# RWKV's inverses in blocks of sixteen rows on VectorE, the samples' blocks turned on chip

## The chip, the cores and the metric

One Trainium2 chip, one core. The metric is the device time of one execution in microseconds (us); the kernel before has a median of 1343.44 us over 3 runs. Engines are called by their names in the profile: PE (TensorE's matmuls), PEld (its weight loads), DVE (VectorE), ACT (ScalarE), POOL (GpSimd), SP (SyncE, from whose queue nearly all DMAs are issued). Each engine takes its instructions in order.

## The reference: one step of a two-layer recurrent decoder

A prompt of 256 tokens and 8 samples of 8 tokens each (320 columns together) run through two layers with the same float32 weights. Layer 0 mixes with 4 GLA heads and 16 RWKV-7 heads, layer 1 with RG-LRU blocks and Mamba-2 heads; each layer ends with a gated feed-forward part of width 2816. Outputs are the tokens' final vectors and all new recurrent states.

The change touches RWKV-7 alone. Its reference is a scan over time, per head with a 64x64 state S:

```python
sa = einsum('bhij,bhj->bhi', s, -kk_t)
s = s * w_t + sa[..., None] * (kk_t * a_t) + v_t[..., None] * k_t
y = einsum('bhij,bhj->bhi', s, r_t)
```

In chunks of 64 tokens this becomes products of matrices, if for each head and chunk a 64x64 triangular system is solved: with A the strictly triangular matrix of the products of the chunk's vectors kk and kk * a (with decays), the chunk needs T = (I + A)^-1. The prompt has 4 chunks and 16 heads, that is 64 inverses of 64x64; the 8 samples have blocks of 8x8, 128 of them.

## The kernel before, in words

All activations lie with channels on the 128 partitions and the 320 tokens along the free axis. A projection (`lin`, L98) streams 320 columns against 128x128 weight tiles; float32 weights and activations are each split into a rounded high part and a remainder, and three matmuls are added up. ScalarE makes the weights' high part (`whi`, L87), VectorE the remainder (`wlo`, L92), from tiles that the sync queue loads (`wraw`, three buffers). So VectorE's queue feeds every projection.

Layer 0 takes the 16 RWKV heads in four quarters of four. Each quarter has `rwkv_front` (six projections, decays, and for two pairs of heads the products of the chunk's vectors), `rwkv_back` (samples, inverse, scan over the four chunks, norm), and beside them one GLA head. The front of the next quarter and the GLA head are written behind a quarter's back; the order on each engine is then laid out at compile time by a scheduler with estimated durations, and does not change at run time. Most of a quarter's tiles (`GA`, `GS`, `BKt`, `SV`, `G`) have one buffer: the next quarter's are written when this quarter's scan has read them.

The path that the change touches, per quarter (4 heads x 4 chunks = 16 matrices):

- `rwkv_pair` writes the 16 matrices into `GA` (128 partitions, 64 columns of time, 32 places for matrices), each twice: VectorE multiplies the product with the mask, GpSimd copies it to a second place (L653 to L655). `GS` takes the samples' blocks.
- `rwkv_inverse_s` (samples): VectorE sums the masked blocks into 64x32 values (L686), two DMAs through DRAM (`usd`) turn them so that 32 partitions hold one 8x8 block each, `solve` substitutes back in 7 pairs of a product and a sum, three DMAs through DRAM (`xsd`) turn the result back, and two products with a mask (`mkb`) spread it to `Ts` (`rts`).
- `rwkv_inverse` (prompt): two block transposes (L712) put each matrix's two diagonal blocks of 32 rows on partitions, one block per partition; ScalarE copies them to the other 64 partitions (L87), so that each partition half solves for half of the columns. Odd rows are folded into even ones (two instructions on 128x512), so that two rows go at a time: 16 steps, each a product `T` (L92) and a sum over its last axis into `X` (L726), from 32 to 512 columns. The result is transposed back (L728), copied into `Tt` by VectorE and GpSimd (eight copies, L738), and the block below the diagonal is joined on TensorE: two transposes (L743), 16 products of 32x32 with `GA`, ScalarE's evacuation, 16 products with `Tt`, ScalarE's evacuation into `Tt`.
- `rwkv_prompt` then runs the four chunks with `Tt` on TensorE.

A float32 matmul of this kernel shows as two records of PE.

Of the kernel before, what the change touches and what calls it, by code (L numbers as in the profile page):

```python
# [23 lines left out]
NB = 8  # L24
# [7 lines left out]
class Net:  # L32
# [370 lines left out]
    def masks0(self, pool):  # L403
        nc = self.nc

        mp = self.t(pool, [P, 2, 64], "mkp")
        msm = self.t(pool, [P, 2, 64], "mks")
        nc.gpsimd.memset(mp, 1.0)
        nc.gpsimd.memset(msm, 1.0)
        for b in (0, 64):  # L410
            for m in (mp, msm):
                self.sel(m[b:b + 64], [[1, 2], [1, 64]], -1, -1)
            self.sel(msm[b:b + 64].rearrange("p a (b t) -> p a b t", t=8), [[0, 2], [-8, 8], [0, 8]], 0, 1)
        self.mkp, self.mks = mp, msm
# [12 lines left out]
        self.eye = self.t(pool, [P, 32, 8], "eye")  # L427
        e1 = self.t(self.m0, [P, 512], "T", 1)[:, :256].rearrange("p (s c) -> p s c", c=8)
        for d, e in enumerate((self.eye, e1)):
            nc.gpsimd.memset(e, 0.0)  # L430
            for r in range(0, P, 32):
                x = e[r:r + 32]
                self.sel(x, [[1, 32], [-1, 8]], -16 * (r // 64) - 8 * d, 0, 1.0, OP.not_equal)
                self.sel(x, [[0, 32], [0, 8]], -16 if d else 15, 1 if d else -1)
        self.tt(self.eye, self.eye, e1, OP.add, nc.gpsimd)
# [102 lines left out]
    def rwkv_front(self, quarter, h, W):  # L538
        q = type("Quarter", (), {})()
        q.n = quarter  # L540
        t = lambda tag, w, n=1: self.t(self.m0, [P, 2, w], tag, self.BUFS.get(tag, n))
        q.AR = t("AR", 640).rearrange("p m (c a t) -> p m c a t", c=5, a=2)
        q.BKt = t("BKt", 640).rearrange("p m (c k) -> p m c k", c=5)
        q.SV = t("SV", 640).rearrange("p m (c k) -> p m c k", c=5)
        q.G = t("G", 640).rearrange("p m (c h t) -> p m c h t", c=5, h=2)

        q.GA = self.t(self.m0, [P, 64, 32], "GA", self.BUFS.get("GA", 1))
        q.GS = self.t(self.m0, [P, 2, 2, 64], "GS", 1)
        q.BV = t("BV", 320).rearrange("p m (c v) -> p m c v", c=5)
# [27 lines left out]
    def rwkv_pair(self, q, m, i, h, W, kr, kn):  # L577
# [60 lines left out]
        for lo, n in ((0, 4), (4, 1)):  # L638
# [7 lines left out]
            for hh in range(2):  # L646
# [31 lines left out]

    def rwkv_inverse_s(self, q):

        nc = self.nc
        usd = self.t(self.dr, [2, 2, 64, 8], "usd", 2)
        xsd = self.t(self.dr, [2, 2, 64, 8], "xsd", 2)
        t = self.t(self.m0, [P, 256], "ti", 1)
        us, U, X, xr, T = (t[:64, 0:32], t[:32, 64:128], t[:32, 128:192], t[:, 32:48], t[:32, 192:256])
# [7 lines left out]
        x3 = xr.rearrange("p (m t) -> p m t", m=2)  # L693
        for hh in range(2):
            self.dq.dma_start(out=x3[hh * 64:hh * 64 + 64], in_=xsd[:, hh].rearrange("m s t -> s m t"))
        q.Ts = self.t(self.m0, [P, 2, 64], "rts", 1)
        for m in range(2):
            self.tt(q.Ts[:, m, :].rearrange("p (b t) -> p b t", t=8),
                    x3[:, m, :].unsqueeze(1).to_broadcast([P, 8, 8]),
                    self.mkb.unsqueeze(2).to_broadcast([P, 8, 8]), OP.mult)  # L700

    def rwkv_inverse(self, q):

        nc = self.nc
        U = self.t(self.m0, [P, 32, 32], "U", 1)
        X = self.t(self.m0, [P, 32, 8], "X", 1)
# [7 lines left out]
        t3 = T.rearrange("p (t m) -> p t m", m=16)  # L716
        self.tt(t3, U[:, :, 1::2], Uf[:, 32::66].unsqueeze(1).to_broadcast([P, 32, 16]), OP.mult)
        self.tt(U[:, :, 0::2], U[:, :, 0::2], t3, OP.subtract)
        nc.gpsimd.memset(Uf[:, 0::33], -1.0)  # L719
        nc.gpsimd.tensor_copy(X, self.eye)  # L720
        for i in range(30, -1, -2):
            k = 32 - i
# [4 lines left out]
        XT = U.rearrange("p t s -> p (t s)")[:, :256].rearrange("p (t g) -> p t g", g=32)  # L727
        nc.vector.transpose(XT, X.rearrange("p s t -> p t s"))  # L728
        q.Tt = Tt = self.t(self.m0, [P, 2, 4, 64], "Tt", 1)
        for a in range(2):  # L730
            for b in range(2):
                src = XT[a * 64 + b * 32:a * 64 + b * 32 + 32].rearrange("p t (b g h) -> p h g b t", b=2, h=2)
                for hh in range(2):
                    o = hh * 64 + b * 32
                    c = b * 32 + a * 16
                    d = Tt[o:o + 32].rearrange("p m c t -> p (m c) t")[:, :, c:c + 16]
                    d = d.rearrange("p g (b t) -> p g b t", b=2)
                    (nc.gpsimd if hh else nc.vector).tensor_copy(d, src[:, hh])  # L738
# [939 lines left out]
```

## Time and profile before

| | |
|---|---|
| timed runs | 1343.44 us median (1339.86, 1343.44, 1346.21) |
| profiled execution | 1337.24 us, span 1335.5 us, mean granted clock 0.961 |
| busy | PE 93%, PEld 84%, DVE 67%, ACT 53%, POOL 15% |
| chain that ended last | PE 74%, DVE 12%, ACT 6%, issue 4%, DMA 2%, POOL 2% |
| on that chain, by line | T L92 1%, X L726 1%, wlo L92 2% |
| T L92, X L726 | 64 each, 44.9 and 27.5 us busy |

Busy shares are means over the whole span. Layer 0's four quarters lie between 95 and 500 us; the two feed-forward parts, in which PE runs almost without a gap, at 557 to 800 and from 1040 on. The chain is followed back from the last instruction, so a line's share there is time that it held the end up, in this execution. A busy PE counts pipelined matmuls.

### The profile page before, as it was taken

The numbers are of one execution on the slowest core, as the hardware profiler recorded it, in microseconds if no ns is written. First come the engines' busy times: TensorE is split into PE (matmuls) and PEld (weight loads), VectorE is DVE, ScalarE is ACT, GpSimd is POOL, SyncE is SP. The second block draws the span as 40 slices with busy tenths as digits, with TensorE's granted clock in tenths as the row PEclk, the third lists the DMA queues.
The fourth block names the chain that finished last, engine by engine and source line by source line (L and its number), as shares of the span: only waits on it lengthen the run. The fifth ranks groups of instructions, "written<-read, shape, count | busy, mean of one in ns | idle before, by whom it ended". The sixth has DMA issues, their size and how long they took to land.

```text
span 1335.5 us, 23851 instructions
## 1 busy us (share of the span) xinstructions
PE 1244.3 (93%) x8909; PEld 1119.8 (84%) x8909; DVE 890.0 (67%) x1925; ACT 710.6 (53%) x1422; POOL 195.1 (15%) x338
## 2 busy tenths in 40 slices
PE   6986998899999999989999999689999999999997
PEld 4874776678678679989999989568888999999997
DVE  5878577869868756765554448987777776555443
ACT  5854353556555454644444456646676564444443
POOL 6332111321311100200000101431111010000010
PEclk9997896999999999999999999789999999999998
DMA  6421423324423436455554545445545545555542
GB/s 180 129 74 31 109 60 96 94 68 119 120 68 111 112 101 182 120 158 148 149 150 141 152 134 149 114 114 139 160 125 156 171 134 160 148 153 146 148 139 82
DMA packets 324801, 168.39 MB, mean 126 GB/s; under 512 B 32492, under 2 KB 323134, under 8 KB 324430
## 3 DMA queue, kind: packets, MB, share of 16 engines
q1 hardware_dynamic: 324462, 166.33, 44.1%
q8 instruction: 70, 1.15, 0.4%
q10 hardware_dynamic: 224, 0.54, 0.1%
q14 instruction: 45, 0.37, 0.1%
HBM read 150.89 MB, written 15.94 MB: 125 GB/s over the span
## 4 chain that ended last, share of the span: by engine, by line
PE 74%; DVE 12%; ACT 6%; issue 4%; DMA 2%; POOL 2%; SPq 0%; DVEq 0%; ACTq 0%; POOLq 0%
PE acc L98 38%; PE bx L98 24%; PE mx L98 9%; PE mx L102 2%; DVE wlo L92 2%; DVE T L92 1%; ACT L87 1%; DMA wraw<-in_w_ffn_up_dram 1%; DMA wraw<-in_w_in_dram 1%; ACT whi L87 1%; DVE cy L95 1%; DVE g L95 1%; DVE g L92 1%; DVE X L726 1%; PE bx L102 0%
## 5 line engine op out<-in xcount | busy, mean ns | idle before, releaser
L98 PE MATMUL acc<-sp,whi 128*128 128x320 f32 (+1 forms) x2192 | 525.8, 323 | 11.4 <-DVE gg L95 3.7
L87 ACT ACTIVATE whi<-wraw 128x512 fp32r<-128x512 f32 (+1 forms) x512 | 314.3, 621 | 384.7 <-PE acc L98 237.5
L92 DVE TENSOR_TENSOR wlo<-wraw,whi 128x512 fp32r<-128x512 f32 (+1 forms) x512 | 350.3, 693 | 236.3 <-ACT whi L87 228.1
L98 PEld LDWEIGHTS acc<-sp,whi 128*128 128x128 f32 (+1 forms) x2192 | 377.6, 192 | 30.2 <-issue 6.7
L98 PE MATMUL acc<-sp,wlo 128*128 128x320 f32 (+1 forms) x1096 | 352.7, 323 | 10.1 <-DVE wlo L92 10.1
L98 PEld LDWEIGHTS acc<-sp,wlo 128*128 128x128 f32 (+1 forms) x1096 | 210.8, 192 | 21.9 <-DVE wlo L92 13.0
L98 PE MATMUL bx<-sp,whi 128*128 128x320 f32 x912 | 208.1, 315 | 0.9 <-ACT sp L87 0.9
L98 PEld LDWEIGHTS bx<-sp,whi 128*128 128x128 f32 x912 | 155.1, 191 | 2.2 <-ACT sp L87 1.5
L98 PE MATMUL bx<-sp,wlo 128*128 128x320 f32 x456 | 144.1, 316 | 0.0
L98 PE MATMUL acc<-fz,whi 128*128 128x320 f32 x440 | 97.3, 310 | 0.0
L98 PEld LDWEIGHTS bx<-sp,wlo 128*128 128x128 f32 x456 | 87.1, 191 | 0.6 <-issue 0.2
L92 POOL TENSOR_TENSOR ft<-ft,ft 128x320 f32<-128x320 f32 x12 | 12.2, 1020 | 451.0 <-ACT ft L87 451.0
L98 PEld LDWEIGHTS acc<-fz,whi 128*128 128x128 f32 x440 | 73.5, 188 | 0.0
L98 PE MATMUL acc<-fz,wlo 128*128 128x320 f32 x220 | 67.9, 309 | 0.0
L98 PE MATMUL bx<-fz,whi 128*128 128x320 f32 x264 | 58.3, 309 | 0.0
L92 DVE TENSOR_TENSOR T<-X,U 128x32 f32<-128x32 f32 (+7 forms) x64 | 44.9, 702 | 0.7 <-POOL U L719 0.3
L98 PEld LDWEIGHTS bx<-fz,whi 128*128 128x128 f32 x264 | 44.1, 188 | 0.0
L98 PEld LDWEIGHTS acc<-fz,wlo 128*128 128x128 f32 x220 | 41.3, 188 | 0.0
L98 PE MATMUL bx<-fz,wlo 128*128 128x320 f32 x132 | 40.7, 308 | 0.0
L87 ACT ACT_TABLE_LOAD x24 | 30.8, 1283 | 2.7 <-issue 2.3
L92 POOL TENSOR_TENSOR g<-g,g 128x320 f32<-128x320 f32 x12 | 11.4, 948 | 116.9 <-ACT g L87 116.9
L726 DVE TENSOR_REDUCE X<-T 128x16 f32<-128x32 f32 (+7 forms) x64 | 27.5, 430 | 0.3
(501 smaller groups left out, 1877.5 us busy)
## 6 DMA issues: line engine op xcount, KB each, us to landing
wraw<-in_w_in_dram SPq DMA_DIRECT2D x86, 512.0 KB
wraw<-in_w_ffn_gate_dram SPq DMA_DIRECT2D x44, 512.0 KB
wraw<-in_w_ffn_up_dram SPq DMA_DIRECT2D x44, 512.0 KB
wraw<-in_w_out_dram SPq DMA_DIRECT2D x32, 512.0 KB
wraw<-in_w_ffn_down_dram SPq DMA_DIRECT2D x32, 512.0 KB
wraw<-in_w_ffn_down_dram SPq DMA_DIRECT2D x16, 384.0 KB
out_dram<-s SPq DMA_DIRECT2D x9, 512.0 KB
S<-in_state_gla_dram SPq DMA_DIRECT2D x16, 256.0 KB
```

The lines of the kernel that those rows point to most:

```text
L87: self.nc.scalar.activation(out, in_, f, scale=scale)
L92: (eng or self.nc.vector).tensor_tensor(out, a, b, op=op)
L95: self.nc.vector.scalar_tensor_tensor(out, a, s, b, op0=op0, op1=op1)
L98: self.nc.tensor.matmul(out, l, r, start=start, stop=stop)
L102: self.nc.tensor.transpose(out, in_, self.ident[:k, :k])
L726: nc.vector.tensor_reduce(X[:, i:i + 2, :], t4, axis=AX.X, op=OP.add, negate=True)
```

## The change

- The inverse works on diagonal blocks of 16 rows instead of 32, so `GA` has 16 places instead of 32 and GpSimd's second copy goes. Two transposes of half the columns put them on partitions; VectorE combines two halves with a column mask (`half`) and copies the result to the other partitions. Eight steps of two rows remain, with 32 to 256 columns; `X` has 16 rows.
- The result is multiplied with `half` before it is transposed back. The copies into `Tt` stay eight.
- A new join of 16-row blocks to 32-row blocks: four transposes, 32 products of 32x32 with `GA`, a product with a mask (`quar`) out of PSUM, 32 products with `Tt`, four subtractions out of PSUM into `Tt`. Its products alternate between partitions 0 and 32, then between all four groups of 32. The old join to 64 rows follows as it was.
- The samples' blocks are turned by VectorE: two transposes, two sums, an addition; then `solve` as before; then a product with a mask (`seq`), two transposes and four copies into `Ts`. The five DMAs and both DRAM tiles go.
- `masks0` builds smaller masks.

The core of the diff:

```diff
-        q.GA = self.t(self.m0, [P, 64, 32], "GA", self.BUFS.get("GA", 1))
+        q.GA = self.t(self.m0, [P, 64, 16], "GA", 1)
...
-                    ga = [q.GA[:, :, g:g + 7:2].rearrange("p t c -> p c t") for g in (i * 8 + hh, 16 + i * 8 + hh)]
-                    self.tt(ga[0], zz[:, :, 0, :], mk_(0), OP.mult)
-                    nc.gpsimd.tensor_copy(ga[1], ga[0])
+                    g = i * 8 + hh
+                    self.tt(q.GA[:, :, g:g + 7:2].rearrange("p t c -> p c t"), zz[:, :, 0, :], mk_(0), OP.mult)
...
     def rwkv_inverse_s(self, q):
-        nc.vector.tensor_reduce(us.rearrange("p (g t) -> p g t", t=8),
-                                q.GS[0:64].rearrange("p m h (b t) -> p (m h) t b", t=8), axis=AX.X, op=OP.add)
-        self.dq.dma_start(out=usd.rearrange("m h s t -> s (m h) t"), in_=us.rearrange("p (g t) -> p g t", t=8))
-        self.dq.dma_start(out=U, in_=usd.rearrange("m h (b s) t -> (m h b) (s t)", s=8))
+        for r in range(2):
+            nc.vector.transpose(bt[:, r], q.GS[r * 32:r * 32 + 32].rearrange("p m h (b t) -> p t (m h b)", t=8))
+        b5 = big.rearrange("p (r t b s) -> p r t b s", r=2, t=8, b=4)
+        for r in range(2):
+            nc.vector.tensor_reduce((v(U), v(X))[r].rearrange("p s t -> p t s"),
+                                    b5[:, r].rearrange("p t b s -> p t s b"), axis=AX.X, op=OP.add)
+        self.tt(U, U, X, OP.add)
         self.solve(v(U), v(X), T, 8)
-        self.dq.dma_start(out=xsd.rearrange("m h (b s) t -> (m h b) (s t)", s=8), in_=X)
...
+        self.tt(big.rearrange("p (t b s) -> p t b s", t=8, b=NB),
+                v(X).rearrange("p s t -> p t s").unsqueeze(2).to_broadcast([32, 8, NB, 8]),
+                self.seq.unsqueeze(1).unsqueeze(3).to_broadcast([32, 8, NB, 8]), OP.mult)
...
+            nc.vector.transpose(w[r * 32:r * 32 + 32], big.rearrange("p (t r s) -> p r t s", t=8, r=2)[:, r])
...
+                nc.vector.tensor_copy(q.Ts[hh * 64:hh * 64 + 64, m].rearrange("p (b t) -> p t b", t=8), w[:, :, g:g + 8])

     def rwkv_inverse(self, q):
-        for b in range(2):
-            r = slice(b * 32, b * 32 + 32)
-            nc.vector.transpose(U[r], q.GA[r, r, :])
-        self.act(U[64:128], U[0:64], AF.Copy)
...
+        for r in range(2):
+            x = slice(r * 32, r * 32 + 32)
+            nc.vector.transpose(A3[x], q.GA[x, x, :].rearrange("p (h j) g -> p j h g", h=2))
...
+        self.stt(U[0:64], A3[0:64, :, 0:16], self.half[0:64, 0:1], A3[0:64, :, 16:32], OP.mult, OP.add)
+        nc.vector.tensor_copy(U[64:128], U[0:64])
...
-        for i in range(30, -1, -2):
+        for i in range(14, -1, -2):
...
+        for hh in range(2):
+            for r in range(2):
+                o = hh * 64 + r * 32
+                nc.vector.transpose(DT[r * 32:r * 32 + 32, hh], Tg[o:o + 32, :, r * 32:r * 32 + 32])
...
+        z = self.bx()
+        for mc in range(8):
+            for hh in range(2):
+                for r in range(2):
+                    o = hh * 64 + r * 32
+                    x = slice(r * 32, r * 32 + 32)
+                    self.mm(z[o:o + 32, mc * 32:mc * 32 + 32], q.GA[x, x, mc * 2 + hh],
+                            DT[x, hh, mc, :])
+        self.tt(Mp.rearrange("p (g t) -> p g t", g=8), z[:, :256].rearrange("p (g t) -> p g t", g=8),
+                self.quar.unsqueeze(1).to_broadcast([P, 8, 32]), OP.mult)
+        z = self.bx()
+        for mc in range(8):
+            for hh in range(2):
+                for r in range(2):
+                    o = hh * 64 + r * 32
+                    self.mm(z[o:o + 32, mc * 32:mc * 32 + 32], Mp[o:o + 32, mc * 32:mc * 32 + 32],
+                            Tg[o:o + 32, mc, r * 32:r * 32 + 32])
+        zg = z[:, :256].rearrange("p (g t) -> p g t", g=8)
+        for hh in range(2):
+            for r in range(2):
+                o = hh * 64 + r * 32
+                d = Tg[o:o + 32, :, r * 32 + 16:r * 32 + 32]
+                self.tt(d, d, zg[o:o + 32, :, 16:32], OP.subtract)
```

## Rows read from the trace of the kernel before

**Rows 1.** The page: busy time, share and instructions of each engine.

```profile
PE 1244.3 (93%) x8909; PEld 1119.8 (84%) x8909; DVE 890.0 (67%) x1925; ACT 710.6 (53%) x1422; POOL 195.1 (15%) x338
```

**Rows 2.** Stretches: start:end, length, each engine's busy us, granted clock, DMA.

```profile
95.00:500.00 405.00, 371.53 (x2965) 291.36 (x2965) 305.04 (x715) 205.11 (x441) 69.47 (x114) 0.93 0.32 89
...
95.00:147.00 52.00, 38.68 (x255) 28.95 (x254) 44.23 (x101) 20.99 (x39) 13.48 (x22) 0.82 0.23 58
190.00:257.00 67.00, 58.03 (x417) 44.89 (x417) 51.41 (x115) 31.81 (x67) 12.56 (x22) 0.82 0.34 94
296.00:360.00 64.00, 60.97 (x501) 48.99 (x501) 57.66 (x129) 38.04 (x79) 14.86 (x23) 1.00 0.38 107
404.00:461.00 57.00, 53.90 (x456) 43.99 (x455) 49.34 (x114) 26.98 (x64) 7.07 (x10) 1.00 0.38 106
```

**Rows 3.** Chain of waits, 95 to 202 us: shares by line.

```profile
by line: PE acc L98 27.5%; PE bx L98 20.1%; PE mx L98 14.2%; DVE T L92 5.9%; issue 4.2%; DVE X L726 2.9%; PE mx L102 2.3%; DVE b L92 1.9%; ACT L87 1.7%; POOL sg L92 1.7%; DVE wlo L92 1.7%; PE bx L102 1.6%; DVE Tt L738 1.6%; POOL b L92 1.5%;
```

**Rows 4.** DVE's groups by shape, 95 to 462: out<-in, count, busy, mean ns, idle.

```profile
L712 DVE STREAM_TRANSPOSE U<-GA 32x1024 f32<-32x1024 f32 x8 | 9.9, 1233 | 1.1 <-POOL GA L655 0.9
...
L92 DVE TENSOR_TENSOR G<-mx,mkp 128x256 f32<-128x256 f32 x12 | 5.0, 417 | 5.4 <-PE mx L98 5.4
...
L92 DVE TENSOR_TENSOR T<-X,U 128x512 f32<-128x512 f32 x4 | 4.7, 1167 | 0.0
L92 DVE TENSOR_TENSOR T<-U 128x512 f32<-128x512 f32 x4 | 4.6, 1142 | 1.1 <-ACT U L87 1.1
...
L743 DVE STREAM_TRANSPOSE U<-Tt 32x256 f32<-32x256 f32 x8 | 3.5, 432 | 0.2
...
L92 DVE TENSOR_TENSOR T<-X,U 128x288 f32<-128x288 f32 x4 | 2.8, 693 | 0.1
L92 DVE TENSOR_TENSOR U<-U,T 128x512 f32<-128x512 f32 x4 | 2.8, 690 | 0.0
...
L726 DVE TENSOR_REDUCE X<-T 128x16 f32<-128x512 f32 x4 | 2.7, 673 | 0.0
L92 DVE TENSOR_TENSOR rw<-bx,rs 128x128 f32<-128x128 f32 x9 | 2.6, 292 | 8.6 <-PE bx L98 8.4
...
L686 DVE TENSOR_REDUCE ti<-GS 64x32 f32<-64x256 f32 x4 | 2.4, 606 | 0.0
...
L726 DVE TENSOR_REDUCE X<-T 128x16 f32<-128x288 f32 x4 | 1.8, 445 | 0.0
...
L858 DVE COPY ryz<-bx 128x64 f32<-128x64 f32 x6 | 1.3, 211 | 0.4 <-ACT rw L87 0.4
```

**Rows 5.** PE in order of time, the join's two rounds in the third quarter.

```profile
355.57 1.22 PE L98 MATMUL bx<-U,GA 32*32 32x32 f32 x32
...
358.16 0.69 PE L98 MATMUL bx<-Tt,U 32*32 32x32 f32 x30
```

**Rows 6.** In order of time: the join's start and end, first and third quarter.

```profile
140.26 0.90 DVE L743 STREAM_TRANSPOSE U<-Tt 32x256 f32<-32x256 f32 x2
...
145.89 0.77 ACT L87 ACTIVATE Tt<-bx 32x256 f32<-32x256 f32 x2 [1.73 <-PE bx L98]
...
343.65 0.90 DVE L743 STREAM_TRANSPOSE U<-Tt 32x256 f32<-32x256 f32 x2
...
358.89 0.77 ACT L87 ACTIVATE Tt<-bx 32x256 f32<-32x256 f32 x2 [0.42 <-PE bx L98]
```

**Rows 7.** In order of time: the samples' two trips through DRAM, first quarter.

```profile
97.53 0.64 SPq L688 DMA_DIRECT2D usd<-ti  x1
...
102.89 0.14 DVE L92 TENSOR_TENSOR ti<-ti 32x1 f32<-32x1 f32 x1
...
109.19 0.34 SPq L692 DMA_DIRECT2D xsd<-ti  x1
...
116.82 0.35 DVE L92 TENSOR_TENSOR rts<-ti,mkb 128x64 f32<-128x64 f32 x2
```

**Rows 8.** POOL in order of time, at the start of layer 0.

```profile
30.95 0.55 POOL L448 COPY prev<-shT 128x8 f32<-128x8 f32 x1 [6.51 <-ACT prev L87]
```

More of the change, by code (lines that the diff above doesn't have):

```diff
@@ L426, in masks0 @@
         self.bones = bo
[L427 to L435, printed above, removed]
+        self.eye = self.t(pool, [P, 16, 8], "eye")
+        nc.gpsimd.memset(self.eye, 0.0)
+        for a in range(2):
+            self.sel(self.eye[a * 64:a * 64 + 64], [[1, 16], [-1, 8]], -8 * a, 0, 1.0, OP.not_equal)
+        self.half = self.t(pool, [P, 2], "half")
+        self.quar = self.t(pool, [P, 32], "quar")
+        nc.gpsimd.memset(self.half, 1.0)
+        nc.gpsimd.memset(self.quar, 1.0)
+        for r in range(0, P, 32):
+            self.sel(self.half[r:r + 32, 0:1], [[0, 1]], 15, -1)
+            self.sel(self.half[r:r + 32, 1:2], [[0, 1]], -16, 1)
+            self.sel(self.quar[r:r + 32], [[0, 32]], -16, 1)
+            self.sel(self.quar[r:r + 32], [[-1, 32]], 15, 0)
+        self.seq = self.t(pool, [32, NB], "seq")
+        nc.gpsimd.memset(self.seq, 0.0)
+        for g in range(4):
+            self.sel(self.seq, [[-1, NB]], -8 * g, 1, 1.0, OP.not_equal)
         self.rst = self.t(pool, [P, NT], "rst")
@@ L681, in rwkv_inverse_s @@
         nc = self.nc
[L682 to L685, printed above, removed]
-        nc.vector.tensor_reduce(us.rearrange("p (g t) -> p g t", t=8),
-                                q.GS[0:64].rearrange("p m h (b t) -> p (m h) t b", t=8), axis=AX.X, op=OP.add)
-        self.dq.dma_start(out=usd.rearrange("m h s t -> s (m h) t"), in_=us.rearrange("p (g t) -> p g t", t=8))
@@ L689, in rwkv_inverse_s @@
-        self.dq.dma_start(out=U, in_=usd.rearrange("m h (b s) t -> (m h b) (s t)", s=8))
-        v = lambda x: x.rearrange("p (s t) -> p s t", t=8)
-        self.solve(v(U), v(X), T, 8)
-        self.dq.dma_start(out=xsd.rearrange("m h (b s) t -> (m h b) (s t)", s=8), in_=X)
-        x3 = xr.rearrange("p (m t) -> p m t", m=2)
-        for hh in range(2):
-            self.dq.dma_start(out=x3[hh * 64:hh * 64 + 64], in_=xsd[:, hh].rearrange("m s t -> s m t"))
-        q.Ts = self.t(self.m0, [P, 2, 64], "rts", 1)
@@ L697, in rwkv_inverse_s @@
[L697 to L700, printed above, removed]
+        t = self.t(self.m0, [64, 704], "ti", 1)
+        big = t[:32, 0:512]
+        U, X, T = t[:32, 512:576], t[:32, 576:640], t[:32, 640:704]
+        v = lambda x: x.rearrange("p (s t) -> p s t", t=8)
+        bt = big.rearrange("p (r t c) -> p r t c", r=2, t=8)
@@ L702, in rwkv_inverse @@
+        w = self.t(self.m0, [64, 256], "ro", 1).rearrange("p (t g) -> p t g", t=8)
+        for r in range(2):
+            nc.vector.transpose(w[r * 32:r * 32 + 32], big.rearrange("p (t r s) -> p r t s", t=8, r=2)[:, r])
+        q.Ts = self.t(self.m0, [P, 2, 64], "rts", 1)
+        for hh in range(2):
+            for m in range(2):
+                g = (2 * m + hh) * 8
+                nc.vector.tensor_copy(q.Ts[hh * 64:hh * 64 + 64, m].rearrange("p (b t) -> p t b", t=8), w[:, :, g:g + 8])
     def rwkv_inverse(self, q):
@@ L706, in rwkv_inverse @@
         nc = self.nc
-        U = self.t(self.m0, [P, 32, 32], "U", 1)
-        X = self.t(self.m0, [P, 32, 8], "X", 1)
+        A = self.t(self.m0, [P, 512], "UA", 1)
         T = self.t(self.m0, [P, 512], "T", 1)
-        for b in range(2):
-            r = slice(b * 32, b * 32 + 32)
-            nc.vector.transpose(U[r], q.GA[r, r, :])
-        self.act(U[64:128], U[0:64], AF.Copy)
+        U = self.t(self.m0, [P, 16, 16], "U", 1)
+        X = self.t(self.m0, [P, 16, 8], "X", 1)
         Uf = U.rearrange("p t s -> p (t s)")
-        t3 = T.rearrange("p (t m) -> p t m", m=16)
@@ L717, in rwkv_inverse @@
-        self.tt(t3, U[:, :, 1::2], Uf[:, 32::66].unsqueeze(1).to_broadcast([P, 32, 16]), OP.mult)
+        A3 = A.rearrange("p (t s) -> p t s", s=32)
+        for r in range(2):
[3 more added lines that the diff above has]
+        nc.vector.tensor_copy(U[64:128], U[0:64])
+        t3 = T[:, :128].rearrange("p (t m) -> p t m", m=8)
@@ L718, in rwkv_inverse @@
+        self.tt(t3, U[:, :, 1::2], Uf[:, 16::34].unsqueeze(1).to_broadcast([P, 16, 8]), OP.mult)
         self.tt(U[:, :, 0::2], U[:, :, 0::2], t3, OP.subtract)
-        nc.gpsimd.memset(Uf[:, 0::33], -1.0)
+        nc.vector.memset(Uf[:, 0::17], -1.0)
         nc.gpsimd.tensor_copy(X, self.eye)
-        for i in range(30, -1, -2):
-            k = 32 - i
+        for i in range(14, -1, -2):
+            k = 16 - i
             t4 = T[:, :16 * k].rearrange("p (i c j) -> p i c j", i=2, c=8)
@@ L726, in rwkv_inverse @@
             nc.vector.tensor_reduce(X[:, i:i + 2, :], t4, axis=AX.X, op=OP.add, negate=True)
-        XT = U.rearrange("p t s -> p (t s)")[:, :256].rearrange("p (t g) -> p t g", g=32)
-        nc.vector.transpose(XT, X.rearrange("p s t -> p t s"))
-        q.Tt = Tt = self.t(self.m0, [P, 2, 4, 64], "Tt", 1)
[L730 to L738, printed above, removed]
+        Xs, XT = A[:, 0:256], A[:, 256:512].rearrange("p (t g) -> p t g", g=32)
@@ L739, in rwkv_inverse @@
+        self.tt(Xs.rearrange("p (c h s) -> p c h s", c=8, h=2),
+                X.rearrange("p s c -> p c s").unsqueeze(2).to_broadcast([P, 8, 2, 16]),
+                self.half.unsqueeze(1).unsqueeze(3).to_broadcast([P, 8, 2, 16]), OP.mult)
+        nc.vector.transpose(XT, Xs.rearrange("p (c s) -> p c s", s=32))
+        q.Tt = Tt = self.t(self.m0, [P, 2, 4, 64], "Tt", 1)
+        Tg = Tt.rearrange("p m c t -> p (m c) t")
         for hh in range(2):
             nc.gpsimd.memset(Tt[hh * 64 + 32:hh * 64 + 64, :, :, 0:32], 0.0)
-        T1 = U[0:32].rearrange("p t s -> p (t s)")[:, 256:768].rearrange("p (h g t) -> p h g t", h=2, g=8)
@@ L742, in rwkv_inverse @@
-        for hh in range(2):
-            nc.vector.transpose(T1[:, hh], Tt[hh * 64:hh * 64 + 32, :, :, 0:32].rearrange("p m c t -> p (m c) t"))
-        Mp = U.rearrange("p t s -> p (t s)")[:, 768:1024]
+        for a in range(2):
+            for r in range(2):
+                src = XT[a * 64 + r * 32:a * 64 + r * 32 + 32].rearrange("p t (b g h) -> p h g b t", b=2, h=2)
+                for hh in range(2):
+                    o = hh * 64 + r * 32
+                    d = Tg[o:o + 32, :, r * 32:r * 32 + 32].rearrange("p g (b a t) -> p g b a t", b=2, a=2)[:, :, :, a]
+                    (nc.gpsimd if hh else nc.vector).tensor_copy(d, src[:, hh])
@@ new lines, in rwkv_inverse @@
+        DT = T[0:64].rearrange("p (h g t) -> p h g t", h=2, g=8)
+        for hh in range(2):
+            for r in range(2):
+                o = hh * 64 + r * 32
+                nc.vector.transpose(DT[r * 32:r * 32 + 32, hh], Tg[o:o + 32, :, r * 32:r * 32 + 32])
+        Mp = Uf
+        z = self.bx()
[6 more added lines that the diff above has]
+                            DT[x, hh, mc, :])
@@ new lines, in rwkv_inverse @@
+        self.tt(Mp.rearrange("p (g t) -> p g t", g=8), z[:, :256].rearrange("p (g t) -> p g t", g=8),
[3 more added lines that the diff above has]
+            for hh in range(2):
+                for r in range(2):
+                    o = hh * 64 + r * 32
+                    self.mm(z[o:o + 32, mc * 32:mc * 32 + 32], Mp[o:o + 32, mc * 32:mc * 32 + 32],
+                            Tg[o:o + 32, mc, r * 32:r * 32 + 32])
@@ L745, in rwkv_inverse @@
+        zg = z[:, :256].rearrange("p (g t) -> p g t", g=8)
+        for hh in range(2):
+            for r in range(2):
+                o = hh * 64 + r * 32
+                d = Tg[o:o + 32, :, r * 32 + 16:r * 32 + 32]
+                self.tt(d, d, zg[o:o + 32, :, 16:32], OP.subtract)
+        T1 = A[0:32].rearrange("p (h g t) -> p h g t", h=2, g=8)
+        for hh in range(2):
+            nc.vector.transpose(T1[:, hh], Tg[hh * 64:hh * 64 + 32, :, 0:32])
         z = self.bx()
```

## The prediction

> **What bounds the kernel now.** I read the busy shares first, then the busy time by stretches, the chain of waits for the first quarter of layer 0, VectorE's groups kept apart by shape, and single instructions in order of time. The page has TensorE at 93% and VectorE at 67% of the span [rows 1], which looks as if an edit on VectorE could bring nothing. The stretches say otherwise. The change touches only RWKV's part of layer 0, 95 to 500 us, which runs in four quarters. There TensorE is busy 371.5 of 405 us at a granted clock of 0.93, and VectorE 305.0 [rows 2]. From the moment a quarter's matrices are there until its inverse is done, the four stretches last 52, 67, 64 and 57 us, 240 together; VectorE is busy 202.6 of them (84%), TensorE 211.6 (88%), and in the first two the granted clock is 0.82, a mean of its two levels (1.2 and 2.4 GHz), in the last two 1.00, the upper one throughout [rows 2]. So in these stretches VectorE is nearly as full as TensorE, and in the first one (44.2 of 52 us, against TensorE's 38.7) fuller. The chain of waits for the first quarter shows the same: products and projections first, but VectorE's back substitution (T at L92, 5.9%, X at L726, 2.9%) and its copies (Tt, 1.6%) hold 10% of it [rows 3]. Neither engine alone sets the length; the chain matrices, inverse, scan, next quarter's matrices does, and VectorE's first-in-first-out queue stretches its first half.
>
> **The change, per quarter.** *What the inverse loses on VectorE.* Sixteen step pairs become eight, and the eight that go are the long ones: the products run from 0.693 us (128x288) to 1.167 (128x512), the sums from 0.445 to 0.673 [rows 4]; by the means of first and last, 8 x 0.930 + 8 x 0.559 = 11.9 us. The two block transposes, 1.233 each at 1024 columns, have 512 now; by columns, a third of the way from the 0.432 of the 256-column one [rows 4], that is 0.70, which saves 1.07. The pair that folds odd rows in (1.142 + 0.690 on 128x512 [rows 4]) works on 128x128, where the nearest row of this size is 0.292 [rows 4]; at 0.35 + 0.29 it saves 1.19. Together 14.2 us.
>
> *What it gains.* A combine on 64x256 and two products with masks on 128x256 at the 0.417 of that size: 1.25. A copy of 64x256 and a memset, between 0.2 (the small copy, 0.211) and 0.7: I take 0.45. Four more transposes of 256 columns: 4 x 0.432 = 1.73. Four subtractions out of PSUM at 0.292: 1.17 [rows 4]. Together 4.6. Net for the inverse: 9.6 us less. ScalarE and GpSimd each lose a copy; neither is late enough anywhere to be counted.
>
> *The samples' blocks.* Before: one sum (0.606) and two products that spread the result (0.35 for both) [rows 4, 7], 0.96. After: four transposes (1.73), two sums (at 0.606, 1.21), an addition (between 0.14 and 0.292; 0.2), a product on 32x512 (between 0.690 and 1.142; 0.69, since the operands are small), and four copies of 64x64 (0.211 each, 0.84) [rows 4, 7]: 4.67. Net 3.7 us more on VectorE; the solve itself stays. For it five small DMAs go. In the first quarter the trip through DRAM lies between the issue at 97.53 and the solve's first product at 102.89, and again between 109.19 and the product at 116.82 [rows 7]: 13.0 us of waiting, in which VectorE did the prompt's steps. I count nothing for that, since the work that covered it is what the inverse needs anyway; that it is worth more is a rival below. The sync queue loses 20 issues, among them waits for VectorE's sum in front of weight loads. I give these nothing either: weight loads run three buffers ahead; if they were late, it would be in that rival.
>
> VectorE's net is then 9.6 - 3.7 = 5.9 us a quarter, 23.6 us in all.
>
> *What is added on TensorE.* A quarter gets two more rounds of 32 small products, each of two records. Before, the first round (all from partitions 0 to 31) takes 1.22 us for 32 records, the second, which goes between partitions 32 and 96, 0.69 for 30 [rows 5]: 0.076 or 0.046 us a product, so 64 of them cost 2.9 to 4.9 us. They differ in two ways, though: the slow one also loads its weights from GA with a stride, the quick one from dense rows. The first new round alternates the partitions and keeps a stride; it could be either. I take 0.046 for one and 0.06 for the other, 3.4 us a quarter.
>
> The Trainium skill, "TensorE: Matmul & The Clock Gate", section "Part 3: Packing small matmuls — row/col tiling", says that a weight load overlaps a running matmul only where the two use different row groups. By that rule both new rounds go at the quick row's price, 2.9 us; by the other reading, in which the stride is what costs, the first goes at the slow one's, 3.9 us, and the total of the change would move by 4 us at most.
>
> That product time matters less than the rounds' latency. The old two rounds, from the end of the last transpose to the end of the last copy, take 5.5 us in the first quarter (141.16 to 146.66) and 15.1 in the third (344.55 to 359.66), where TensorE's queue held projections in front of them [rows 6]. Without ScalarE's two evacuations (0.78 + 0.77; the new rounds' are in VectorE's sum already) that is 3.9 to 13.5 us. I take 4.9, near the short end, since in the third quarter TensorE was not idle while the round waited. Part of that is covered by VectorE's other work, which has a backlog of weight splits: over the four stretches it is busy 84%; right behind a finished inverse I assume a little over half, so 2.1 us a quarter is not covered, 8.4 in all.
>
> *The start.* The masks that go are GpSimd's, before 25 us; later it is idle 6.51 us until ScalarE gives it the next operand [rows 8], so the shorter setup is worth nothing. GA is now read until the third round instead of the first; its next writer comes behind the scan, which waits for the inverse anyhow: nothing.
>
> **Sum.** 23.6 saved on VectorE, taken at its full worth as the stretches are mostly VectorE's, less 8.4: 15.2 us. The profiled execution took 1337.24 us (span 1335.5, 1.7 around it), below all three timed runs (median 1343.44, lowest 1339.86). 1337.2 - 15.2 = 1322.0, 1.1% less; on the median that is 1328.
>
> **Rivals.**
> *No change (0.20).* TensorE is the bound of quarters three and four: 61.0 of 64 and 53.9 of 57 us busy at clock 1.00 [rows 2]. Then only the first two quarters gain 3.8 each, and the other two pay 3.4 each for the new products: -0.8 us, 1343. Against it: busy there counts pipelined matmuls, and the chain still has 10% of VectorE in the quarter where it is visible.
> *Slower (0.16).* Each new round queues behind projections, as the old ones did in the third quarter. A quarter then pays 13.5 - 5.9 = 7.6 us. With two of four like that and two as forecast (-3.8): +7.6, 1351; with all four +30, 1374. It decides from the point at which the two new rounds cost over 5.9 us uncovered. For it speaks that TensorE takes its queue in order and is 88% full here; against it that waiting behind useful work is no idle time.
> *Faster by more (0.16).* The sample's trips through DRAM were what TensorE waited for, and the sync queue's waits held weights back. In quarters one and two the granted clock is 0.82, and in the first TensorE is idle 13 of 52 us; if 8 of the 13.0 us count in each of these two, the sum is -31 us, 1312.
>
> **From cases to numbers.** The forecast has 0.48, with its own range 1318 to 1336 (an error of the rounds from 2 to 4 us a quarter and of the unshown VectorE prices of 1 to 2). A difference below 0.5%, 6.7 us, can't be told from none. Faster by more than that, below 1336.7: 0.45 of the forecast, all 0.16 of the last rival, 0.02 of the first: 0.63. Within it: 0.22 (0.03, 0.17 and 0.02). Slower: 0.15. The range runs from 1305 (the DRAM rival and a little more) to 1353 (two bad quarters); about 0.08 lies below and 0.10 above.
>
> **What would show it.** Right: 32 products T and 32 sums X instead of 64 each, some 13 and 9 us; VectorE some 24 us less in 95 to 500; the stretch from GA's transpose to the last write of Tt shorter by 3 to 5 us in each quarter; both new rounds near 1.5 us of matmuls. Wrong on the rounds: more than 4 us between the end of a transpose and its subtraction, with VectorE idle. Wrong on the bound: VectorE lighter as said and 95 to 500 as long as before, with TensorE's clock at 1.00 and busy. Wrong altogether: the new sample steps in front of the inverse's own in VectorE's queue, so that GA's transposes to the first step take longer than the eight steps save.

## The result and the profile after

The changed kernel takes 1333.03 us (median of 17 runs, 1322.87 to 1338.72), the kernel before on the same chip 1339.86 (17 runs). The ratio is 0.9933, 95% interval 0.9907 to 0.996: faster by 0.67%, about 9 us. The forecast was 15 us less, 1328. The direction and the own range hold; the experiments show that both terms that gave the 15 were too hopeful, the saving put too large and the price too small, and that most of what came in the end is the clock's, which no term forecast. The profiled execution took 1333.28 us, span 1331.6, granted clock 0.959.

The page of after, busy time by engine, for [rows 1]:

```profile
PE 1252.8 (94%) x9421; PEld 1127.3 (85%) x9421; DVE 866.9 (65%) x1949; ACT 707.6 (53%) x1419; POOL 174.6 (13%) x325
```

VectorE lost 23.1 us of busy time (890.0 before), where 23.6 were forecast. TensorE gained 8.5 us and 512 records, the four quarters' 64 new products of two records each. The stretches of after, for [rows 2]; columns as there. The four short ones run from GA's last write to the last write of Tt, in whole us:

```profile
95.00:500.00 405.00, 383.66 (x3524) 302.59 (x3524) 287.73 (x743) 203.23 (x441) 56.39 (x99) 0.93 0.34 90
97.00:141.00 44.00, 35.29 (x369) 26.72 (x370) 39.69 (x106) 18.78 (x36) 11.16 (x19) 0.92 0.27 61
182.00:247.00 65.00, 60.25 (x564) 46.54 (x563) 47.20 (x126) 32.21 (x70) 10.66 (x20) 0.87 0.39 105
292.00:358.00 66.00, 64.28 (x624) 51.79 (x623) 55.75 (x141) 37.92 (x81) 14.70 (x23) 0.97 0.46 120
397.00:461.00 64.00, 61.87 (x624) 50.42 (x624) 48.78 (x133) 28.97 (x69) 6.31 (x11) 0.98 0.42 111
```

They last 44, 65, 66 and 64 us (52, 67, 64, 57 before): 239 against 240. In these rows VectorE has 11 us less, TensorE 10 more, and it is now busy 221.7 of 239. The last stretch of [rows 2] begins only with GA's transpose, 3 us after GA's last write. Between the same two events the four last 51.6, 67.9, 63.2 and 59.7 us before and 43.5, 64.8, 66.1 and 63.2 after, 242 against 238. Quarter one alone became much shorter. The chain of waits from 95 to 188 us, for [rows 3], as far as the view shows it:

```profile
by line: PE acc L98 21.3%; PE bx L98 21.0%; PE mx L98 13.5%; issue 4.5%; DVE wlo L92 3.7%; POOL b L92 2.7%; DVE ti L92 2.4%; ACT SV L87 2.2%; DVE T L92 2.1%; DVE T L772 1.9%; DVE kk L95 1.8%; DVE Tt L766 1.7%; PE mx L102 1.5%; DVE UA L734 1
```

The back substitution T is 2.1% of it (5.9% before). VectorE's groups by shape, 95 to 500 us, for [rows 4]:

```profile
L772 DVE STREAM_TRANSPOSE T<-Tt 32x256 f32<-32x256 f32 x16 | 7.0, 434 | 0.5
...
L734 DVE STREAM_TRANSPOSE UA<-GA 32x512 f32<-32x512 f32 x8 | 5.5, 689 | 0.1
...
L700 DVE STREAM_TRANSPOSE ti<-GS 32x256 f32<-32x256 f32 x8 | 5.0, 621 | 0.1
...
L703 DVE TENSOR_REDUCE ti<-ti 32x64 f32<-32x256 f32 x8 | 4.7, 617 | 0.1
...
L92 DVE TENSOR_TENSOR Tt<-Tt,bx 32x128 f32<-32x128 f32 x16 | 4.5, 284 | 4.4 <-PE bx L98 4.1
...
L92 DVE TENSOR_TENSOR ti<-ti,seq 32x512 f32<-32x512 f32 x4 | 4.4, 1094 | 0.0
...
L92 DVE TENSOR_TENSOR UA<-X,half 128x256 f32<-128x256 f32 x4 | 2.5, 636 | 0.1
```

The join of the third quarter, TensorE in order of time (start, us), for [rows 5] and [rows 6]; the granted clock is 1.00 here:

```profile
347.58 0.60 PE L102 MATMUL bx<-ident,b 128*128 128x128 f32 x4
348.11 1.15 PE L98 MATMUL bx<-T,GA 32*32 32x32 f32 x64
...
350.11 0.75 PE L98 MATMUL bx<-Tt,U 32*32 32x32 f32 x64
...
353.55 0.26 PE L98 MATMUL bx<-UA,GA 32*32 32x32 f32 x2 [0.30 <-DVE UA L799]
...
354.23 1.11 PE L98 MATMUL bx<-UA,GA 32*32 32x32 f32 x30
...
356.20 0.24 PE L98 MATMUL bx<-Tt,U 32*32 32x32 f32 x2
...
356.72 0.69 PE L98 MATMUL bx<-Tt,U 32*32 32x32 f32 x30
...
358.07 0.68 PE L98 MATMUL bx<-BV,Tt 64*64 64x64 f32 x8
```

VectorE's side of this join is done far ahead of it:

```profile
327.21 1.83 DVE L772 STREAM_TRANSPOSE T<-Tt 32x256 f32<-32x256 f32 x4
```

It ends at 329.0, and the first new product starts at 348.1, right behind the samples' last transposes (`ident,b`). The same wait is 16.5 us in quarter two (to 232.8) and 19 in quarter four (to 450.9); quarter one has none. This looks like the whole answer, and was my first theory. It is not.

**Where the time went.** The change can act only until the first feed-forward part begins (first product with `fr`: 555.84 us before, 552.23 after; 3.6 of the 3.9 us between the spans). From 78 us to there, the kernel before, then after:

```profile
78.00:555.84 477.84, 440.30 (x3462) 355.81 (x3461) 348.89 (x802) 242.63 (x513) 84.96 (x147) 0.94 0.35 99
```

```profile
78.00:552.23 474.23, 449.16 (x3986) 363.56 (x3985) 330.82 (x831) 240.22 (x511) 70.64 (x130) 0.94 0.37 99
```

Length less PE busy is TensorE's idle time: 37.5 before, 25.1 after. The trace's clock records show 58.0 and 56.4 us at the lower level (by the row, 2 x 0.06 x length = 57), of which TensorE was busy 53.1 and 55.2; half of that, 26.5 and 27.6, is what this level cost. What is left is its work at the upper level. The split is an estimate: the work of kernels with the same matmuls should come out the same, but for the orders and banks of the kernel before that are tried below (e7, e8, e11, e12) it gives 404 to 410 us where the kernel before has 413.7, so a few us of a difference in this column can be the split's own.

| 78 us to the feed-forward part | length | idle | cost of the lower level | work |
|---|---|---|---|---|
| before | 477.8 | 37.5 | 26.5 | 413.7 |
| after | 474.2 | 25.1 | 27.6 | 421.6 |
| half of the steps left out (e1) | 448.3 | 19.8 | 15.6 | 412.9 |
| new join left out (e2) | 447.8 | 24.5 | 10.3 | 412.9 |
| after, acc 2 banks (e9) | 486.4 | 32.6 | 32.5 | 421.3 |
| the same, join in its own bank (e10) | 491.9 | 29.5 | 39.3 | 423.1 |

So in the profiles: 12.4 us less idle time, 7.9 more work, 1.1 more for the clock. For the timed runs each result lists span and clock; span x clock is an estimate of the time at the upper level, the rest that of the lower level's cost (time in which TensorE idles at the lower level counts here too). Means and ratios leave out runs over 1.5% above the fastest of their kernel (one of e1's six, one of e3's twelve, two of e4's six, two of e5's twelve, one of e11's six, one of the 17 of before beside e9 to e12), while the time given first under each experiment is the median of all its runs. Means with 95% intervals (Student's t, as some have only four runs):

| kernel (runs) | span | at the upper level | cost of the lower level |
|---|---|---|---|
| before (17, beside e1 to e4) | 1338.9 | 1279.1 ±1.8 | 59.8 ±4.1 |
| after (17) | 1330.1 | 1276.4 ±1.0 | 53.8 ±3.0 |
| e1 (5) | 1312.9 | 1264.5 ±3.0 | 48.3 ±9.4 |
| e2 (4) | 1305.8 | 1268.9 ±2.1 | 36.9 ±1.0 |
| e3 (11) | 1332.5 | 1274.5 ±2.2 | 57.9 ±5.0 |
| e4 (4) | 1363.6 | 1282.5 ±4.4 | 81.2 ±11.3 |
| e5 (10) | 1349.8 | 1289.5 ±1.4 | 60.2 ±4.2 |
| e6 (12) | 1354.0 | 1285.5 ±1.3 | 68.5 ±3.3 |
| e7 (6) | 1395.5 | 1299.4 ±3.1 | 96.1 ±6.7 |
| e8 (6) | 1400.2 | 1290.7 ±3.1 | 109.5 ±6.7 |
| e9 (12) | 1351.5 | 1290.4 ±1.3 | 61.1 ±4.5 |
| e10 (6) | 1356.0 | 1286.8 ±2.4 | 69.2 ±5.2 |
| e11 (5) | 1361.2 | 1283.6 ±3.5 | 77.6 ±8.5 |
| e12 (6) | 1359.2 | 1283.6 ±1.2 | 75.7 ±7.0 |

The kernel before gave 1279.5 to 1279.9 and 60.2 to 61.9 on the other two occasions. Of the 9 us, about 3 (2.7 ±2.1) are at the upper level and 6 (±5) the clock's; the second is barely clear of the noise.

### The profile page after: what moved, and what is told of

Read it like the earlier page. It is cut to its first block, busy times and chain, and to the rows that moved or that the text cites. A ratio compares the mean times of both kernels' runs of the same rounds, so it can differ in the third digit from the quotient of the medians.

```text
span 1331.6 us, 24876 instructions
## 1 busy us (share of the span) xinstructions
PE 1252.8 (94%) x9421; PEld 1127.3 (85%) x9421; DVE 866.9 (65%) x1949; ACT 707.6 (53%) x1419; POOL 174.6 (13%) x325
## 4 chain that ended last, share of the span: by engine, by line
PE 75%; DVE 13%; ACT 4%; issue 3%; DMA 3%; POOL 2%; SPq 0%; DVEq 0%; ACTq 0%; POOLq 0%
PE acc L98 38%; PE bx L98 25%; PE mx L98 9%; PE mx L102 2%; DVE wlo L92 2%; DMA wraw<-in_w_ffn_up_dram 1%; DVE cy L95 1%; DVE S L95 1%; DVE g L95 1%; DVE g L92 1%; DVE T L92 0%; DVE b L92 0%; PE bx L102 0%; DMA wraw<-in_w_in_dram 0%; DMA s<-csd 0%
## 5 line engine op out<-in xcount | busy, mean ns | idle before, releaser
L92 DVE TENSOR_TENSOR wlo<-wraw,whi 128x512 fp32r<-128x512 f32 (+1 forms) x512 | 346.5, 685 | 239.4 <-ACT whi L87 231.2
L98 PE MATMUL acc<-fz,wlo 128*128 128x320 f32 x220 | 67.9, 308 | 0.0
L98 PEld LDWEIGHTS bx<-fz,wlo 128*128 128x128 f32 x132 | 24.8, 188 | 0.0
L92 DVE TENSOR_TENSOR x<-x,acc 128x320 f32<-128x320 f32 x30 | 14.5, 483 | 12.3 <-PE acc L98 12.3
```

The source lines that it names most:

```text
L92: (eng or self.nc.vector).tensor_tensor(out, a, b, op=op)
L98: self.nc.tensor.matmul(out, l, r, start=start, stop=stop)
```

## The experiments

Ratios are to the kernel before, on the same chip.

**e1: what is a microsecond of the long steps worth?** In the kernel before, eight of sixteen step pairs are left out, the long ones.

```diff
-        for i in range(30, -1, -2):
+        for i in range(30, 14, -2):
```

> The kernel before with the eight long step pairs of the prompt's inverse left out (that part isn't computed): some 48 us of VectorE less, nothing else touched. Theory A (every us off VectorE counts, as the forecast had it): about -45 us. Theory B (the join waits for the samples' products, because both take the two bx banks in the order of the program; VectorE's steps are late only in quarters one and two): about -17 us, -10 from the first quarter, -7 from the second, nothing from the third and fourth, where the join already comes right behind the samples' last transposes. Theory C (TensorE is full in these quarters): less than -5 us.

Measured 1316.62, ratio 0.9794 (0.9756 to 0.9832): 27.6 us less for some 48 us of VectorE by the instructions' lengths (11.9 a quarter; its page has 846.1 us busy, 43.9 less). Its row in the view of 78 us to the feed-forward part:

```profile
78.00:526.29 448.29, 428.52 (x3469) 349.84 (x3467) 306.25 (x742) 242.88 (x514) 82.58 (x148) 0.96 0.39 105
```

Idle time fell by 17.7 us, the lower level's cost by 10.9, work stayed. So the steps do count, at some 0.6 of their length, and over a third of that is the clock (in the timed runs 14.6 ±3.5 us at the upper level and 11.5 ±10 by the clock).

**e2: what do the two new rounds cost?** The changed kernel without them (four transposes, 64 products, product with `quar`, four subtractions); the blocks of 16 are not joined to 32.

```diff
-        DT = T[0:64].rearrange("p (h g t) -> p h g t", h=2, g=8)
...
-                self.tt(d, d, zg[o:o + 32, :, 16:32], OP.subtract)
```

> The changed kernel without the new 16-row join (its four transposes, 64 products, mask product and four subtractions are left out): Theory B: the rounds begin only when the samples are done and so lie fully on the path: 4 to 7 us a quarter, about -20 us. Theory A: only VectorE's share counts, 3.3 us a quarter: -13 us. Theory C: TensorE's time for 64 products, about 2 us a quarter: -8 us.

Measured 1307.51, ratio 0.974 (0.9709 to 0.977): against after, 26 us less, more than any theory gave. Its row in the same view:

```profile
78.00:525.76 447.76, 423.22 (x3470) 344.21 (x3468) 318.84 (x794) 244.15 (x514) 72.23 (x130) 0.97 0.39 105
```

Idle time is that of after (24.5 and 25.1): VectorE's share of the join, some 3.3 us a quarter, and the rounds' latency cost TensorE nothing. Work is 8.7 us less, and the lower level's cost 17.3 less (27.3 us at this level, 56.4 in after). The timed runs say the same: 7.5 ±2.3 and 16.9 ±3.2. So the join costs its products' work, and with it goes twice as much by the clock. The second quarter shows most of the latter; stretches of after:

```profile
214.00:233.00 19.00, 17.15 (x139) 12.03 (x138) 13.56 (x28) 11.34 (x24) 5.12 (x8) 1.00 0.41 102
233.00:247.00 14.00, 14.00 (x220) 10.87 (x217) 6.24 (x15) 5.82 (x13) 1.93 (x3) 0.51 0.37 78
247.00:257.00 10.00, 10.00 (x65) 7.43 (x65) 4.25 (x10) 3.95 (x12) 1.51 (x3) 0.50 0.19 52
```

and without the new rounds, over the same part of the quarter:

```profile
210.00:222.00 12.00, 11.66 (x77) 7.95 (x76) 8.84 (x16) 9.68 (x19) 3.72 (x5) 1.00 0.44 119
222.00:232.00 10.00, 10.00 (x123) 7.48 (x121) 6.68 (x14) 6.57 (x17) 2.46 (x4) 1.00 0.53 105
232.00:240.00 8.00, 8.00 (x104) 6.04 (x102) 5.04 (x13) 2.58 (x8) 1.19 (x2) 1.00 0.71 169
```

In after TensorE idles 1.79 us before 232.27, then does the samples' transposes and the first of the two rounds:

```profile
232.27 0.63 PE L102 MATMUL bx<-ident,b 128*128 128x128 f32 x4 [1.79 <-DVE b L92]
232.82 1.17 PE L98 MATMUL bx<-T,GA 32*32 32x32 f32 x64
```

From 233 on its clock is at the lower level (1.2 GHz) for 24 us with PE busy throughout. Three such stretches lie at joins (128 to 134, 233 to 257, 459 to 472 us) and make 44 of the 56 us, but only that of quarter two begins in a new round. Windows of after at the other two:

```profile
127.00:128.00 1.00, 0.00 (x0) 0.00 (x0) 0.94 (x3) 0.00 (x0) 0.90 (x3) 0.78 0.69 106
128.00:134.00 6.00, 5.28 (x135) 4.39 (x136) 5.03 (x12) 0.00 (x0) 0.06 (x1) 0.50 0.53 125
450.00:458.00 8.00, 7.90 (x189) 6.10 (x188) 4.55 (x16) 4.01 (x15) 0.00 (x0) 1.00 0.37 61
459.00:472.00 13.00, 13.00 (x110) 8.90 (x106) 1.06 (x3) 2.77 (x10) 0.00 (x0) 0.50 0.12 37
```

In quarter one the level falls between 127 and 128 us, in which TensorE does nothing, and the first product starts at 128.3. In quarter four the new rounds (451 to 454 us) pass at 1.00, and the level falls in the last round of the old join. The join of quarter three passes at 1.00. And without the new rounds the first quarter has a longer such stretch, not a shorter one:

```profile
123.00:135.00 12.00, 8.00 (x85) 5.55 (x85) 9.72 (x23) 3.07 (x8) 2.44 (x6) 0.50 0.39 83
```

So that the join's removal brings the clock's 17 us is measured; that the 64 products as such lower the clock is not shown. The scheduler also lays out the rest in another order, and below an order alone moves the lower level's cost by 36 and 49 us (e7, e8). No run separates the products from the idle time in front of them or from the order.

**e3: the samples alone, taken back.** The changed kernel with the samples' blocks through DRAM, as before.

```diff
-            nc.vector.transpose(bt[:, r], q.GS[r * 32:r * 32 + 32].rearrange("p m h (b t) -> p t (m h b)", t=8))
...
+        self.dq.dma_start(out=usd.rearrange("m h s t -> s (m h) t"), in_=us.rearrange("p (g t) -> p g t", t=8))
```

> The changed kernel with the samples' blocks turned through DRAM as before (inverse as changed). VectorE has about 15 us less to do, the samples' result comes some 6 us later. Theory A: -13 us. Theory B: +2 to +6 us, since the samples' path is the late one in the first quarter and has slack elsewhere. Theory C: within 3 us.

Measured 1333.91, ratio 0.9952 (0.9916 to 0.9987), which can't be told from after. Its row, to the feed-forward part again:

```profile
78.00:555.84 477.84, 452.05 (x3986) 366.74 (x3985) 315.41 (x795) 240.13 (x511) 70.56 (x128) 0.93 0.37 99
```

VectorE has 15.4 us less to do there than in after, and TensorE's idle time is the same (25.8 and 25.1). So the idle time that the change saves is saved by the inverse alone, and taking the samples off VectorE or off DRAM changes nothing net. In after `Ts` is begun 6 to 27 us earlier than in the kernel before (110.9, 201.6, 310.3 and 414.7 us against 116.8, 228.1, 323.9 and 426.5), but TensorE came to the product with it at 217.8, 336.5 and 440.9 us in the last three quarters, over 15 us after it was there. That fits trips through DRAM [rows 7] that were mostly hidden. It is not shown for each quarter: in e3 the product came within 1 us of Ts in the first two (120.9 and 229.3 us), so there the samples' path did set its time.

**e4: the samples alone, done.** The kernel before with the samples turned on chip (in a buffer of the norm, since no other was free).

```diff
-        us, U, X, xr, T = (t[:64, 0:32], t[:32, 64:128], t[:32, 128:192], t[:, 32:48], t[:32, 192:256])
+        U, X, T = t[:32, 512:576], t[:32, 576:640], self.t(self.m0, [P, 64], "ti", 1)[:32]
...
+            nc.vector.transpose(bt[:, r], q.GS[r * 32:r * 32 + 32].rearrange("p m h (b t) -> p t (m h b)", t=8))
```

> The kernel before with the samples' blocks turned on chip (in the norm's buffer, for room; inverse as before). VectorE has about 15 us more to do, five DMAs a quarter go. Theory A: +13 us. Theory B: -2 to -6 us from the first quarter. Theory C: within 3 us.

Measured 1371.17, ratio 1.017 (1.0122 to 1.0219): 23 us more, beyond all theories; 3.4 ±4.7 at the upper level, 21 ±12 by the clock. So it is the clock that made it dear; that VectorE, late as it is in this kernel, got more work in front of the inverse is a likely cause, but not a shown one. How much the borrowed buffer adds stays open.

**e5 to e8: another order of a quarter's back.** Inverse, samples, scan (e5 in after, e7 in before), and inverse, scan, samples (e6, e8).

```diff
-        self.rwkv_sample(q)
         self.rwkv_inverse(q)
+        self.rwkv_sample(q)
```

My theory B was that the wait of 16 to 20 us in front of the join ate the gain: the samples, the join and the scan take their PSUM banks from one ring of two (`bx`) in the program's order.

> The changed kernel with the prompt's inverse written in front of the samples' part (one swap of two calls). Theory B (the two bx banks go in the order of the program, so the join's rounds wait for the samples' last transposes): in quarters two to four the time from the last of the four new transposes to the first product, 17 to 19 us now, falls below 5, the rounds run beside the samples' work, and the kernel gains 10 to 25 us on the changed one. Theory C (TensorE's queue is full of projections and the GLA head anyway): the rounds move, the time stays within 4 us. Theory D (VectorE's load alone counts): within 4 us, as no work goes.

> The changed kernel with inverse, scan, then the samples' part. Theory B: the scan follows its inverse at once, 20 us or more off the changed kernel, unless the samples' part, which then holds the single buffers BKt, SV and G, delays the next quarter's matrices by as much. Theory C: within 4 us.

> The kernel before with the same swap. Theory B: there the join comes behind the samples' last transposes only in quarters three and four (waits of 11 and 4 us), so the swap gains 15 us at most, less than in the changed kernel. Theory C: within 4 us.

> The kernel before with inverse, scan, then the samples' part. Theory B: as the swap, a few us more or less by what the samples then delay. Theory C: within 4 us.

Measured 1352.22 (1.0073, 1.0045 to 1.0101), 1355.78 (1.0095, 1.0064 to 1.0126), 1399.05 (1.0401, 1.0363 to 1.0439) and 1400.86 (1.0438, 1.0402 to 1.0474). All are slower, against B. In e6 the scan followed the join at once (242.0 us in quarter two, 247.6 in after), and the samples' product with Ts came at 268.3 instead of 217.8. So the wait moved from the scan to the samples. To the feed-forward part, e6, e7 and e8:

```profile
78.00:571.30 493.30, 453.30 (x4007) 368.33 (x4007) 330.91 (x828) 242.47 (x512) 70.76 (x130) 0.92 0.35 95
```

```profile
78.00:620.13 542.13, 474.01 (x3494) 381.26 (x3492) 345.71 (x803) 245.37 (x515) 82.73 (x148) 0.86 0.31 87
```

```profile
78.00:620.76 542.76, 474.88 (x3501) 383.81 (x3498) 347.80 (x805) 245.54 (x515) 83.98 (x148) 0.85 0.31 87
```

TensorE's idle time rises from 25.1 us in after to 40.0, and from 37.5 in the kernel before to 68, with the same matmuls. The samples' products had covered VectorE's inverse. Without this cover the kernel before loses 4%, after, whose inverse is shorter, 1.4 to 1.6%; much of the 4% is the clock (36 and 49 us of the timed runs).

**e9 to e12: the join out of the ring.** To have a bank for it, the projections' sums (`acc`) get two instead of three: e9 (after) and e11 (before) are these controls, e10 and e12 have the join in the free bank.

```diff
-    PS = 3, 3, 2
+    PS = 2, 3, 2
...
-        z = self.bx()
+        z = self.t(self.ps, [P, 512], "jx", 1)
```

> The changed kernel with two PSUM banks instead of three for the projections' sums (acc); nothing else differs. It is the control for the next run, which gives the bank that came free to the join. Theory B (the samples' part, the join's rounds and the scan share two banks, bx, that are handed out in the order of the program, so that the rounds stand behind the samples' last transposes) says nothing of acc. A projection needs a bank until it is copied out, so I expect 0 to 12 us more than the changed kernel's 1333.

> The run before, with the four rounds of the join in a PSUM bank of their own (jx). The order on VectorE stays; on TensorE the first new round of quarters two to four is now ahead of the samples' product with Ts or right behind it, not behind the samples' last transposes. Theory B: the 16 to 20 us for which VectorE's finished inverse waited in each of these three quarters come down to a few, and the scan is ready when the samples' part ends, so the time falls by 10 to 25 us against the control. Theory C (TensorE is full in these quarters, 60 to 64 of 65 us, so that a wait behind its useful work costs nothing): within 4 us of the control. Theory D (the rounds cost by themselves, by their 128 small products and the evacuations between, wherever they stand): within 4 us as well, and each of the rounds then shows TensorE idle beside it.

> The kernel before with two banks for the projections' sums: the control for the next run. 0 to 12 us more than the kernel before, about as much as the same edit adds to the changed kernel.

> The run before with the join in a bank of its own. In the kernel before VectorE's inverse is late, so that the join waited behind the samples for 10 us in quarter three and 3 in quarter four alone. Theory B: 0 to 8 us less than its control, and the changed kernel's gain over the kernel before is larger in this pair (both with a bank for the join) than in the controls. Theory C and D: within 4 us of the control, and the gain the same in both pairs, 6 to 12 us.

Measured 1352.28 (1.0073, 1.0042 to 1.0104), 1357.36 (1.0102, 1.0069 to 1.0135), 1364.66 (1.0129, 1.0088 to 1.0171) and 1360.38 (1.0127, 1.0085 to 1.0169). A third bank is worth some 18 us, more than expected. The join's own bank gives nothing in time: the intervals of e9 and e10 overlap, and after's gain is no larger in the pair with it (0.25%) than in the controls (0.55%). The edit did what it should; TensorE in e10, third quarter:

```profile
331.68 0.32 PE L98 MATMUL jx<-T,GA 32*32 32x32 f32 x2
...
345.86 0.45 PE L98 MATMUL bx<-rw,rts 64*64 64x64 f32 x8
...
349.84 0.24 PE L98 MATMUL jx<-Tt,U 32*32 32x32 f32 x2
...
351.73 0.63 PE L102 MATMUL bx<-ident,b 128*128 128x128 f32 x4
...
356.80 0.60 PE L102 MATMUL bx<-ident,b 128*128 128x128 f32 x4
357.33 0.44 PE L98 MATMUL bx<-BV,Tt 64*64 64x64 f32 x4
```

The join's products now begin ahead of the samples' product with Ts and end before the last two groups of the samples' transposes; Tt is done at 350.9 us, and the scan starts at 357.3, behind those transposes. At the upper level e10 is 3.6 ±2.7 us faster than e9, and the clock takes 8.1 ±7. The three joins of quarters two to four lie in or at stretches of the lower level (201 to 228, 324 to 341, 440 to 464 us, the last with a break). So theory B falls with its 10 to 25 us, and theory C, that a wait behind useful work of a full TensorE costs within 4 us, holds; of theory D half holds: the join costs by itself, but not by idle time.

No whole version beat the changed kernel.

## Why the prediction came out nearly right

- *VectorE's sum: right.* 23.1 us of 23.6 on the page. By the lengths of the instructions that the edit touches, the inverse saved 9.8 us a quarter (9.6 forecast) and the samples cost 4.5 (3.7 forecast), 21.2 in all. Parts were off in both directions: the samples' new instructions take 5.5 us a quarter instead of 4.67 (the product with `seq` 1.094 instead of 0.69, the transposes with a strided source 0.621 instead of 0.432), GA's transposes 0.689 of the forecast 0.70, the subtractions 0.284 of 0.292.
- *"Taken at its full worth": the step that failed.* The 23.1 us took 12.4 off TensorE's idle time, about half; e1 gives some 0.6 for the long steps, clock included, and the last 15.4 us between after and e3 took off nothing. I saw VectorE at 84% in the four stretches [rows 2] and named neither engine the bound, then counted as if VectorE were. TensorE had 37.5 us of idle time to lose in all.
- *The rounds' 8.4 us: the number of the work, by a wrong way.* I priced latency in front of TensorE; it cost no idle time (e2). The products' work, which the forecast priced at 13.6 us and then left out of the sum for the latency, is what they cost: 7.9 to 8.7 us by the split, 7.6 by the rows of quarter three (1.15 and 0.75). With what the clock lost the join costs 26 us. The prediction had no term for the clock, though [rows 2] showed 0.82 in two stretches.
- *The errors add up, and the clock made up for part of them.* In place of 15.2 us the profiles show 4.5 at the upper level (12.4 of idle time less 7.9 of work), the timed runs 2.7 ±2.1. That 9 us came is owed to the clock, 6 ±5. Without the join the lower level cost 36.9 us (e2) against 59.8 before, so most of what the shorter inverse could have won there was lost again with the join. So that the time came within 5 us of the forecast is in good part luck.
- *A product's price.* At a clock of 1.00 the first round takes 1.15 us for 64 records, 0.036 a product, the second 0.75, 0.023, both below the 0.046 and 0.06. The old first round, all from one group of 32 partitions, still takes 1.11 for 30. This agrees with what the Trainium skill, "TensorE: Matmul & The Clock Gate", section "Part 3: Packing small matmuls — row/col tiling", says of weight loads from different row groups. The rows also decide between the forecast's two readings: the new first round, two groups with a stride, is no dearer (0.036) than the old second, two groups without one (0.69 for 30, 0.046). So it was the group, not the stride, that made the old first round slow.
- *The rivals.* "No change" named TensorE as the bound of quarters three and four; from GA's last write to Tt these two became 3 us longer each, with TensorE busy 126 of 130 us, so its mechanism was there. "Slower" priced the rounds' queueing at 7.6 us a quarter; they queued even longer, for 16 to 19 us, and e10 shows that this cost next to nothing (3.6 us of the whole at the upper level, none in time). "Faster by more" falls with e3.
- *What would show it.* The stretches from GA's first transpose to Tt were to be 3 to 5 us shorter each; they are 8, 3 and 3 shorter (50.9, 67.1 and 62.4 before) and the last 7 longer (56.0 and 62.8). The 32 products and sums take 14.5 and 9.5 us, as forecast.

## What to carry to other kernels

Read the bound as TensorE's idle time, its work and its clock, each by itself, before a VectorE saving is counted: a saving is worth at most the idle time that it removes plus the clock it brings back. A finished operand that waits 20 us in front of a full engine is hardly a loss; small products put on that engine are one. Span x clock of the timed runs separates the clock from the rest, and for most kernels here the part at the upper level has a tighter interval than the time itself.

## What the runs showed of the hardware

In several edits the clock moved more time than the work did. Of e2's 26 us, 17 are the lower level's cost, at the same idle time; e8, which changes an order alone, adds 11 us to the kernel before at the upper level and 49 by the clock. In after, the clock was at its lower level with PE busy 24.0 of 24 us (233 to 257), so a busy PE row does not show that it will stay up. What in a join brings it down is open.
